# Seven edits to a two-block transformer kernel on one core: the head, the transition, a skipped branch, the convolution's tap matrices

## The chip, the cores and the metric

The kernel runs on one core of one Trainium2 chip. A core has five engines with instruction streams of their own: TensorE (PE, matmuls and transposes; PEld is its weight load), VectorE (DVE), ScalarE (ACT), GpSimd (POOL) and SyncE (SP, which here only issues DMAs). They meet at semaphores. Matrices come from HBM by DMA into SBUF; matmul results stand in PSUM. The metric is the device time of one execution in microseconds (us); lower is better. Before the change three runs gave 1420.13, 1415.26 and 1418.39 us, median 1418.39 us.

## What is computed

All of it is float32 on 256 tokens of width 1024. The first block is a recurrent mixer and a block attention side by side, a cross attention to a memory of 256 rows, and a mixture of 32 experts of which each token takes two. The second block has a retention mixer, a feed-forward layer (FFN), a causal depthwise convolution between two dense matrices, and a second FFN:

```
h = rmsnorm(x, norm_mix); x = x + mixers(h @ w_in) @ w_out
x = x + memory_cross_attention(rmsnorm(x, norm_xattn), rmsnorm(mem, mem_norm), ...)
x = x + hierarchical_moe(rmsnorm(x, norm_ffn), ...)        # 32 experts, 6 MB each
x = rmsnorm(x, norm_final)
h = x; h = h + retention_pool_mixer(rms_norm(h), ...)
h = h + swiglu(rms_norm(h), gate, up, down)
h = h + conformer_conv(rms_norm(h), ...)                   # 31 taps per channel, then layer norm and silu
h = h + swiglu(rms_norm(h), ...); return rms_norm(h)
```

## The kernel before

Every dense product is done as three products of a split: a value is kept as `hi` (rounded) plus `lo` (the rest), and hi·hi, lo·hi and hi·lo are summed in PSUM. A weight piece of 1 MB is loaded into a place `raw` (L270), ACT writes its high half `whi` (L305) and DVE its low half `wlo` (L307); a place is loaded again when both are done. SP issues all weight loads in program order from one queue, so a load that waits for its place holds those behind it.

Most of the program is ordered by a scheduler; in regions marked `manual_schedule` the order on the named engines is the order in which the code is written, and `issue_after(x)` puts an instruction behind x.

- **The head** (`start`, L449 to L543). PE does 24 matmuls on zeros, then waits for the first normed input. Four pieces of `x` (2 token tiles `tt`, 2 column halves `c`) are squared on ACT and DVE (`rstd`); POOL multiplies them by the gain (L512); DVE does a reciprocal root in some twenty small steps (`rsqrt`, L208 to L223); ACT (tt 0) and DVE (tt 1) multiply by it (L472, L474); PE transposes (L480), ACT and DVE split (L484, L488), and the first products follow (L502).
- **The transition** (`cross`). While PE ends the mixer's output product `r` (L436 to L438), POOL multiplies `x` by the gain (L1128), the memory `m` by its gain (L1145) and writes two low halves of `w_kv_x` (L307); DVE does the root of m's norm; DVE scales m's first tile (L1147), ACT the second (L1148); PE then transposes m (L1133).
- **The experts** (`experts`, `overflow`). The 192 MB of expert weights stream through some fifteen places. Behind expert 7 every engine reads a count from SBUF and branches (L1631, L1632): if any expert has over 32 tokens, `overflow` redoes the rest, with loads `ow` on SP's queue (L1434, L1436). In the timed run the branch skips it.
- **Tap matrices** (`conv_weights`, L1926). One POOL instruction writes the 128x6144 tile `w` with which PE does six of the eight channel blocks of the convolution. It stands ahead of `ffn(0)`.
- **Entries** (`enter`): how each of the three later layers starts. Behind the last products of the layer before, `add(c, tt)` adds a quarter of the result to `x` (L1041) and multiplies it by the gain into `xg` (L1042), both on DVE; PE transposes `xg` (L1048), and the first products (`first`, L421) follow. The low halves of the layer's first weight are written by POOL, as is one of the second weight.
- **The convolution** (`conformer`). DVE adds up two channel blocks, tap by tap (L1961); PE does the other six (L2050). Sums over channels of values and squares go through `both` on DVE (L1987) to `sums` on PE (L1974); mean and scale follow, then `centred` (L2077), the scale (L2091), silu and the split.

Of the kernel before, what the change touches and what calls it, by code (L numbers as in the profile page):

```python
# [12 lines left out]
OP = mybir.AluOpType  # L13
# [134 lines left out]
class Block:  # L148
# [298 lines left out]
    def start(self):  # L447
# [57 lines left out]
        with self.tc.manual_schedule(engines={DVE, ACT, POOL, PE}):  # L505
            idle = self.gs.tile([128, 128], F32, name="idle")
            nc.vector.memset(idle, 0.0)
            self.warm(24, idle)
            for c in range(2):
                for tt in range(2):  # L510
                    s = slice(c * 512, (c + 1) * 512)
# [6 lines left out]
            wlow(0, 2)  # L518
            t0, t1 = turned(0, 0), turned(1, 0)
            high(t0, 0, 0)  # L520
            high(t1, 1, 0)
            low(t0, 0, 0)
            low(t1, 1, 0)
            wlow(2, 2)
            scale(0, 1)
            scale(1, 1)
# [12 lines left out]
            wlow(4, 4)  # L539
            products(4, 1, 0, last=True)  # L540
# [485 lines left out]
    def enter(self, g, now, then, *rooms):  # L1026

        nc, x = self.nc, self.x
        products, py, early = self.left
        w = self.halves(0, self.load(now), by=nc.gpsimd)  # L1030
        raw = self.load(then)
# [7 lines left out]
        def add(c, tt):  # L1039
            xs = x[:, tt, half(c)]  # L1040
            nc.vector.tensor_tensor(xs, xs, py[c][tt], op=OP.add)  # L1041
            nc.vector.tensor_tensor(xg[:, tt, half(c)], xs, g[:, half(c)], op=OP.mult)  # L1042

# [20 lines left out]
        with self.tc.manual_schedule(engines={PE, ACT, DVE, POOL}):  # L1064
# [17 lines left out]
            products(1, 1)  # L1082
            add(1, 1)
            turn(1, 0)
# [25 lines left out]
    def cross(self):  # L1110
        nc, i, c = self.nc, self.i, self.c
        self.marks = [self.loads[n].ins for n in (-6, -4)]
        last = self.los[-2].ins
        with self.tc.issue_after(self.loads[-4].ins):
# [27 lines left out]
        with self.tc.manual_schedule(engines={PE, ACT, DVE, POOL}):  # L1142
            gained(0, nc.gpsimd)
            rs = self.rstd(m, after=last)
            nc.gpsimd.tensor_tensor(m[:, 1], m[:, 1], gm, op=OP.mult)  # L1145
            w = self.halves(0, wm, by=nc.gpsimd)
            nc.vector.scalar_tensor_tensor(m[:, 0], m[:, 0], rs[:, 0:1], gm, op0=OP.mult, op1=OP.mult)  # L1147
            nc.scalar.activation(m[:, 1], m[:, 1], AF.Copy, scale=rs[:, 1:2])  # L1148
            t = [turned(m, j, tt) for j in range(2) for tt in range(2)]
            for n in range(4):  # L1150
                high(t[n], hm, n // 2, n % 2)
            for n in range(4):
                low(t[n], hm, n // 2, n % 2)
            gained(1, nc.gpsimd)
# [3 lines left out]
            self.part_cols(w, hm, pm, 0, 0, 0)  # L1158
            self.part_cols(w, hm, pm, 0, 0, 1)
# [266 lines left out]
    def overflow(self):  # L1426
# [3 lines left out]
        def load(src, n):  # L1430
            w = self.ye.tile([128, 2048], F32, name="ow", tag="ye")[:, 0:1024].rearrange("p (k c) -> p k c", k=n)
            if n == 8:
                for a in range(2):
                    nc.sync.dma_start(out=w[:, 4 * a:4 * a + 4], in_=src[a * 512:(a + 1) * 512].rearrange("(p k) c -> p k c", k=4))  # L1434
# [435 lines left out]

    def ffn(self, layer):
        nc, i = self.nc, self.i
# [18 lines left out]
        for f in range(n):  # L1891
# [10 lines left out]
            nc.scalar.activation(s, s, AF.Silu)  # L1902
            nc.gpsimd.tensor_tensor(s, s, rb, op=OP.mult)  # L1903
            nc.vector.tensor_tensor(s, s, pu, op=OP.mult)
# [20 lines left out]
    def conv_weights(self):  # L1925

        shape = [128, 32 * len(BY_PE), 32]
        self.w4 = self.wc.tile(shape, F32, name="w4")
        self.nc.gpsimd.tensor_tensor(self.w4, self.v("w_taps").unsqueeze(2).to_broadcast(shape),
                                     self.c("rep4")[:, None].to_broadcast(shape), op=OP.mult)  # L1930

    def conformer(self):
# [70 lines left out]
        with self.tc.manual_schedule(engines={DVE, ACT, POOL}):  # L2003
# [35 lines left out]
            w4 = self.w4.rearrange("p (b q g) c -> p b q g c", b=len(BY_PE), q=8)  # L2039
            some(99)  # L2040
            w2 = self.pieces(self.rows_of("conv_w_pw2_2", 0))
            made = []
            for n, b in enumerate(BY_PE):
                left = len(BY_PE) - 1 - n
                ps = self.bank("cv")[:, 0:256]
                if not left:
                    moments(total, first=True)
# [4 lines left out]
                if not left:  # L2052
                    moments(pair)
                nc.scalar.activation(dw[:, b], ps, AF.Identity, bias=v("b_dw", b))
                pair = dw[:, b], squared(b)
                if left > 1:
                    add([pair])
                if left == 2:
                    add([(dw[:, d], squared(d)) for d in BY_DVE])
                    made += self.halves(*next(w2))  # L2060
# [18 lines left out]
        with self.tc.manual_schedule(engines={PE, DVE, ACT, POOL}):  # L2079
# [7 lines left out]
            biased(1)  # L2087
            centred(0, 2)
            for b0, n in ((0, 1), (1, 1), (2, 2), (4, 2), (6, 2)):
                s = slice(b0, b0 + n)  # L2090
                nc.vector.tensor_tensor(dw[:, s], dw[:, s], scale[:, None].to_broadcast([128, n, 256]), op=OP.mult)  # L2091
                for b in range(b0, b0 + n):
                    nc.scalar.activation(dw[:, b], dw[:, b], AF.Silu, scale=v("ln_g", b), bias=v("ln_b", b))
                if b0 and b0 < 6:
                    centred(b0 + n, 2)
                nc.scalar.activation(hi[:, s], dw[:, s], AF.Copy)
# [3 lines left out]
    def run(self):  # L2100
# [41 lines left out]
        with ExitStack() as c0:  # L2142
# [33 lines left out]
            with ExitStack() as c2:  # L2176
                self.pools(c2, wc=1)
                self.conv_weights()
                with ExitStack() as c1:
                    self.pools(c1, ffa=2)  # L2180
                    self.ffn(0)
# [79 lines left out]
```

## Time and profile before

| | |
|---|---|
| median of three runs | 1418.39 us |
| profiled execution | 1419.03 us, its span 1417.2 us |
| PE, PEld | 1235.8 us busy (87%), 1058.7 us (75%) |
| DVE, ACT, POOL | 741.5 us (52%), 517.2 us (36%), 170.1 us (12%) |
| DMA | 360.19 MB, mean 254 GB/s; 418 to 419 GB/s through most of the expert stage |
| mean granted PE clock | 0.925 |

The stages by the timeline: head 0 to 27.7 us, mixers to 281, cross attention and routing to 355, experts to about 805, retention to 915, FFN to 1100, convolution to 1215, second FFN to 1405, end at 1417. In the profile a busy share is a mean over stages with unlike limits; a row of the timeline names in brackets how long its engine had been idle, and for whom. A granted clock of 1.00 is TensorE at 2.4 GHz, 0.50 at 1.2 GHz.

### The profile page before, as it was taken

The numbers are of one execution on the slowest core, as the hardware profiler recorded it, in microseconds if no ns is written. First come the engines' busy times: TensorE is split into PE (matmuls) and PEld (weight loads), VectorE is DVE, ScalarE is ACT, GpSimd is POOL, SyncE is SP. The second block draws the span as 40 slices with busy tenths as digits, with TensorE's granted clock in tenths as the row PEclk, the third lists the DMA queues.
The fourth block names the chain that finished last, engine by engine and source line by source line (L and its number), as shares of the span: only waits on it lengthen the run. The fifth ranks groups of instructions, "written<-read, shape, count | busy, mean of one in ns | idle before, by whom it ended". The sixth has DMA issues, their size and how long they took to land. (4 is left out here: it accounts for less than half of the span.)

```text
span 1417.2 us, 29773 instructions
## 1 busy us (share of the span) xinstructions
PE 1235.8 (87%) x12864; PEld 1058.7 (75%) x12864; DVE 741.5 (52%) x1460; ACT 517.2 (36%) x802; POOL 170.1 (12%) x132
## 2 busy tenths in 40 slices
PE   7999999999886477776766799799999998999997
PEld 7989889798765355453544498699999975899996
DVE  5487547866332122121222686765555895755555
ACT  4554533454221111111111464344444424544443
POOL 2022201312000000000000220511111200211112
PEclk8999989999998787687788899899999998999999
DMA  6535514996999899999999985355556186655620
GB/s 207 154 120 170 154 39 146 353 368 246 403 418 415 361 418 418 419 419 419 419 418 419 379 307 186 112 197 195 182 179 187 52 203 204 209 179 180 192 90 30
DMA packets 146460, 360.19 MB, mean 254 GB/s; under 512 B 6672, under 2 KB 101904, under 8 KB 121744
## 3 DMA queue, kind: packets, MB, share of 16 engines
q1 hardware_dynamic: 144800, 353.69, 68.0%
q0 software_dynamic: 1376, 4.25, 1.0%
q8 instruction: 103, 1.69, 0.5%
q14 instruction: 37, 0.30, 0.1%
q10 hardware_dynamic: 144, 0.26, 0.0%
HBM read 354.92 MB, written 3.26 MB: 253 GB/s over the span
## 5 line engine op out<-in xcount | busy, mean ns | idle before, releaser
L307 DVE TENSOR_TENSOR wlo<-raw,whi 128x1024 fp32r<-128x1024 f32 x231 | 297.0, 1291 | 193.2 <-ACT whi L305 190.0
L305 ACT ACTIVATE whi<-raw 128x1024 fp32r<-128x1024 f32 x242 | 254.6, 1058 | 319.7 <-issue 77.4
L1539 PE MATMUL gu<-raw,xe 128*32 128x128 f32 x4096 | 164.2, 308 | 51.0 <-DMA raw<-in_w_exp_up_dram 26.5
L1539 PEld LDWEIGHTS gu<-raw,xe 128*32 128x32 f32 x4096 | 128.9, 121 | 86.7 <-DMA raw<-in_w_exp_up_dram 34.1
L1563 DVE SCALAR_TENSOR_TENSOR ye<-dn,gs,ye 32x256 fp32r<-32x256 f32 x128 | 61.5, 481 | 149.0 <-ACT ye L1562 148.4
L1554 PE MATMUL dn<-raw,ht 128*32 128x256 f32 x1024 | 82.2, 451 | 60.2 <-DMA raw<-in_w_exp_down_dram 37.8
L1562 ACT ACTIVATE ye<-dn,gs 32x256 fp32r<-32x256 f32 x128 | 59.7, 466 | 184.2 <-PE dn L1554 109.2
L1554 PEld LDWEIGHTS dn<-raw,ht 128*32 128x32 f32 x1024 | 34.9, 123 | 94.0 <-DMA raw<-in_w_exp_down_dram 31.0
L413 PE MATMUL fu<-hT,whi 128*128 128x256 f32 x352 | 99.7, 283 | 0.0
L414 PE MATMUL fu<-hTl,whi 128*128 128x256 f32 x352 | 99.6, 283 | 0.0
L415 PE MATMUL fu<-hT,wlo 128*128 128x256 f32 x352 | 99.6, 283 | 0.0
L413 PE MATMUL fg<-hT,whi 128*128 128x256 f32 x320 | 90.6, 283 | 0.0
L415 PE MATMUL fg<-hT,wlo 128*128 128x256 f32 x320 | 90.5, 283 | 0.0
L414 PE MATMUL fg<-hTl,whi 128*128 128x256 f32 x320 | 90.5, 283 | 0.0
L1903 POOL TENSOR_TENSOR fs<-fs,r 128x512 f32<-128x512 f32 x22 | 38.5, 1750 | 302.6 <-ACT fs L1902 302.6
L438 PE MATMUL f<-wlo,fa 128*128 128x512 f32 x176 | 69.2, 393 | 0.0
L436 PE MATMUL f<-whi,fa 128*128 128x512 f32 x176 | 68.9, 391 | 0.0
L437 PE MATMUL f<-whi,fa 128*128 128x512 f32 x176 | 68.7, 391 | 0.0
L413 PEld LDWEIGHTS fu<-hT,whi 128*128 128x128 f32 x352 | 67.1, 190 | 0.0
L414 PEld LDWEIGHTS fu<-hTl,whi 128*128 128x128 f32 x352 | 67.0, 190 | 0.0
L415 PEld LDWEIGHTS fu<-hT,wlo 128*128 128x128 f32 x352 | 67.0, 190 | 0.0
L1620 ACT ACTIVATE hd<-gu,scale 128x128 f32<-128x128 f32 x32 | 11.8, 368 | 144.2 <-PE gu L1539 144.2
(620 smaller groups left out, 2846.8 us busy)
## 6 DMA issues: line engine op xcount, KB each, us to landing
raw<-in_w_exp_gate_dram SPq DMA_DIRECT2D x64, 1024.0 KB, 19.9
raw<-in_w_exp_up_dram SPq DMA_DIRECT2D x64, 1024.0 KB, 19.9
raw<-in_w_exp_down_dram SPq DMA_DIRECT2D x63, 1024.0 KB, 19.9
raw<-in_ffn_w_gate_dram SPq DMA_DIRECT2D x22, 1024.0 KB, 5.4
raw<-in_ffn_w_up_dram SPq DMA_DIRECT2D x22, 1024.0 KB, 5.4
raw<-in_ffn_w_down_dram SPq DMA_DIRECT2D x22, 1024.0 KB, 5.0
raw<-in_w_in_dram SPq DMA_DIRECT2D x20, 1024.0 KB, 5.5
raw<-in_conv_w_pw_dram SPq DMA_DIRECT2D x12, 1024.0 KB, 5.5
```

What stands on the lines that cost most here:

```text
L305: nc.scalar.activation(hi, raw[:, k:k + step], AF.Copy)
L307: self.los.append(eng.tensor_tensor(lo, raw[:, k:k + step], hi.bitcast(F32), op=OP.subtract))
L413: nc.tensor.matmul(ps[:, cb], lhsT=whi[:, k, s], rhs=hi[:, k0 + k], start=f, stop=False)
L414: nc.tensor.matmul(ps[:, cb], lhsT=whi[:, k, s], rhs=lo[:, k0 + k], start=False, stop=False)
L415: nc.tensor.matmul(ps[:, cb], lhsT=wlo[:, k, s], rhs=hi[:, k0 + k], start=False, stop=l)
L436: nc.tensor.matmul(ps[tt], lhsT=hi[:, k0 + k, s], rhs=whi[:, k, cols], start=f, stop=False)
L437: nc.tensor.matmul(ps[tt], lhsT=lo[:, k0 + k, s], rhs=whi[:, k, cols], start=False, stop=False)
L438: nc.tensor.matmul(ps[tt], lhsT=hi[:, k0 + k, s], rhs=wlo[:, k, cols], start=False, stop=l)
L1539: nc.tensor.matmul(pg[quarter(n), at:at + 128], lhsT=xe[:, 4 * kh + k], rhs=w[:, k, n // 2, n % 2], start=(at == kh == k == 0), stop=(at > ...
L1554: nc.tensor.matmul(pd[n % 2][quarter(n), 0:256], lhsT=ht[:, quarter(2 * half + k)], rhs=wd[:, k, n * 256:(n + 1) * 256], start=(half + k = ...
L1562: nc.scalar.activation(hi, part, AF.Copy, scale=gs[q])
L1563: nc.vector.scalar_tensor_tensor(lo, part, gs[q], hi.bitcast(F32), op0=OP.mult, op1=OP.subtract)
```

## The change

1. Head: POOL's four gain products and the two kinds of scale become one DVE instruction for each piece, `x * rs * g`; the low halves of the first weight move behind those of the input.
2. Entries: the first weight's second pair of halves (rows 4 to 8) is issued behind the last `add`, ahead of POOL's low half of the second weight.
3. Transition: the gain products, m's gain and the low halves of `w_kv_x` go from POOL to DVE; both tiles of m are scaled on DVE (`scaled`); the root moves ahead of the last two low halves of `w_out`.
4. Overflow: the loads `ow` go from SP's queue to POOL's.
5. Tap matrices: six POOL instructions of 128x1024, one behind POOL's product in each of the steps 2 to 7 of `ffn(0)`.
6. Convolution: two of the ten adds into `both` stand among the taps of the second channel block.
7. `centred` for three of the four block pairs stands ahead of the first scale.

```diff
@@ start: scale(tt, c)
-            if tt:
-                nc.vector.tensor_scalar(xn[:, tt, s], xn[:, tt, s], rs[:, tt:tt + 1], None, op0=OP.mult)
-            else:
-                nc.scalar.activation(xn[:, tt, s], xn[:, tt, s], AF.Copy, scale=rs[:, tt:tt + 1])
+            nc.vector.scalar_tensor_tensor(xn[:, tt, s], self.x[:, tt, s], rs[:, tt:tt + 1], g[:, s], op0=OP.mult,
+                                           op1=OP.mult)
...
-                    nc.gpsimd.tensor_tensor(xn[:, tt, s], self.x[:, tt, s], g[:, s], op=OP.mult)
@@ enter
-        w = self.halves(0, self.load(now), by=nc.gpsimd)
+        of = self.load(now)
+        w = self.halves(0, of[:, 0:4], by=nc.gpsimd)
...
-            add(1, 1)
+            with self.tc.issue_after(add(1, 1)):
+                w += self.halves(4, of[:, 4:8], by=nc.gpsimd)
@@ cross
-        last = self.los[-2].ins
+        last, end = self.los[-3].ins, self.los[-1].ins
...
-            gained(0, nc.gpsimd)
             rs = self.rstd(m, after=last)
-            nc.gpsimd.tensor_tensor(m[:, 1], m[:, 1], gm, op=OP.mult)
-            w = self.halves(0, wm, by=nc.gpsimd)
-            nc.vector.scalar_tensor_tensor(m[:, 0], m[:, 0], rs[:, 0:1], gm, op0=OP.mult, op1=OP.mult)
-            nc.scalar.activation(m[:, 1], m[:, 1], AF.Copy, scale=rs[:, 1:2])
+            with self.tc.issue_after(end):
+                self.scaled(m, rs, gm, m)
+            gained(0, nc.vector)
...
+            rest(*w[0])
+            gained(1, nc.vector)
+            rest(*w[1])
+            self.part_cols(w, hm, pm, 0, 0, 0)
@@ overflow: load
-                nc.sync.dma_start(out=w, in_=src.rearrange("(k p) c -> p k c", p=128))
+                nc.gpsimd.dma_start(out=w, in_=src.rearrange("(k p) c -> p k c", p=128))
@@ ffn
+            if f > 1:
+                with self.tc.issue_after(scaled.ins):
+                    next(beside, None)
@@ conformer
-            some(99)
...
+                some((8, 10, 99)[min(n, 2)])
...
-            centred(0, 2)
+            for b0 in (0, 2, 4):
+                centred(b0, 2)
```

PE's stream keeps its order but for the transition, where the eight transposes of `xg` move behind the first eight products of m. DVE in the transition before, from the adds of the last quarter of the mixer's result (`x<-x,r`) to m's low halves (`mTl`):

```order
L1011 TENSOR_TENSOR x<-x,r 128x512
L307 TENSOR_TENSOR wlo<-raw,whi 128x1024
L1011 TENSOR_TENSOR x<-x,r 128x512
L307 TENSOR_TENSOR wlo<-raw,whi 128x1024 x3
L210 TENSOR_SCALAR rstd<-ms 128x2
...
L222 SCALAR_TENSOR_TENSOR rstd<-rs,rstd 128x1 x2
L1147 SCALAR_TENSOR_TENSOR raw<-raw,rstd 128x1024
L1011 TENSOR_TENSOR x<-x,r 128x512 x2
L1140 TENSOR_TENSOR mTl<-tr,mT 128x4x128 x4
```

In this order the root (L210 to L222) stands behind four low halves, and one tile of m is scaled behind it. DVE in the same place now (L368 is the scaling of m, L1124 the gain product):

```order
L1005 TENSOR_TENSOR x<-x,r 128x512
L307 TENSOR_TENSOR wlo<-raw,whi 128x1024
L210 TENSOR_SCALAR rstd<-ms 128x2
...
L222 SCALAR_TENSOR_TENSOR rstd<-rs,rstd 128x1 x2
L307 TENSOR_TENSOR wlo<-raw,whi 128x1024 x2
L368 SCALAR_TENSOR_TENSOR raw<-raw,rstd 128x1024 x2
L1005 TENSOR_TENSOR x<-x,r 128x512
L1124 TENSOR_TENSOR raw<-x,raw 128x512
L1005 TENSOR_TENSOR x<-x,r 128x512
L1124 TENSOR_TENSOR raw<-x,raw 128x512
L1136 TENSOR_TENSOR mTl<-tr,mT 128x4x128 x4
```

The root stands two low halves earlier, both tiles of m are scaled right behind the last low half, and two gain products (L1124) have come in ahead of m's low halves; two low halves and two more gain products follow these.

SP at the branch before (the body goes on for some 570 loads):

```order
L279 DMA raw<-in_w_exp_gate_dram 128x2048 x2
L279 DMA raw<-in_w_exp_up_dram 128x2048 x2
L1631 TENSOR_LOAD chosen
L1632 COMPARE_AND_BRANCH
L1434 DMA ow<-in_w_exp_gate_dram 128x4x128 x2
```

The body's loads stand here in SP's stream, behind its branch. SP at the same branch now:

```order
L279 DMA raw<-in_w_exp_up_dram 128x2048 x2
L1634 TENSOR_LOAD chosen
L1635 COMPARE_AND_BRANCH
L1635 UNCONDITIONAL_BRANCH x2
L1634 ISA x2
L279 DMA raw<-in_w_exp_down_dram 128x2048 x2
```

SP still reads the count and branches, over an empty body; the loads stand in POOL's stream.

POOL from the retention (`v`) to the convolution's first step before:

```order
L1848 TENSOR_TENSOR v_17726<-v_17726,row 128x1024
L1929 TENSOR_TENSOR w_18228<-vec,cst 128x6144
L307 TENSOR_TENSOR wlo<-raw,whi 128x1024 x3
L1903 TENSOR_TENSOR fs<-fs,r 128x512 x11
L307 TENSOR_TENSOR wlo<-raw,whi 128x1024
```

The long instruction (L1929) stands ahead of the FFN's first low halves. POOL in the same place now:

```order
L1851 TENSOR_TENSOR v_17721<-v_17721,row 128x1024
L307 TENSOR_TENSOR wlo<-raw,whi 128x1024 x3
L1907 TENSOR_TENSOR fs<-fs,r 128x512 x3
L1939 TENSOR_TENSOR w_18741<-vec,cst 128x1024
L1907 TENSOR_TENSOR fs<-fs,r 128x512
L1939 TENSOR_TENSOR w_18741<-vec,cst 128x1024
...
L1907 TENSOR_TENSOR fs<-fs,r 128x512 x3
L307 TENSOR_TENSOR wlo<-raw,whi 128x1024
```

The one long instruction is gone from its place ahead of the FFN's low halves; six short ones stand each behind one of the FFN's products.

## Rows read from the trace of the kernel before

**Rows 1.** Waits of PE, whole run: engine, line, waited for: us, times, longest.
```profile
PE dn L1554 <- DMA raw<-in_w_exp_down_dram: 37.8, 34, 2.7
...
PE sums L1974 <- DVE both L1987: 4.8, 1, 4.8
...
PE tr L1133 <- DVE raw L1147: 3.7, 1, 3.7
```
**Rows 2.** Windows: us; busy us (instructions) of PE, PEld, DVE, ACT, POOL; PEclk, DMA, GB/s.
```profile
12.00:14.00 2.00, 0.00 (x0) 0.00 (x0) 2.00 (x3) 0.00 (x0) 2.00 (x3) 0.81 1.09 348
14.00:23.00 9.00, 6.12 (x27) 5.72 (x28) 5.47 (x14) 4.60 (x7) 1.60 (x4) 0.50 0.64 174
...
450.00:460.00 10.00, 9.35 (x254) 7.93 (x246) 4.00 (x23) 0.73 (x2) 0.00 (x0) 1.00 1.01 419
475.00:485.00 10.00, 0.71 (x8) 0.52 (x12) 1.72 (x4) 1.48 (x4) 0.00 (x0) 0.50 0.56 215
...
902.00:904.00 2.00, 2.00 (x7) 1.52 (x6) 1.38 (x2) 0.00 (x0) 0.00 (x0) 0.50 1.02 354
...
991.00:1008.00 17.00, 17.00 (x123) 16.00 (x122) 9.33 (x9) 7.40 (x8) 1.82 (x1) 1.00 0.56 186
```
**Rows 3.** Timeline of the head: start us, us, engine, line, what [idle before <-releaser].
```profile
9.29 0.17 DVE L210 TENSOR_SCALAR rstd<-ms 128x2 int32<-128x2 int32 x1
...
9.87 4.92 POOL L512 TENSOR_TENSOR xn<-x,row 128x512 f32<-128x512 f32 x4 [6.34 <-DMA row<-in_norm_mix_dram]
...
15.42 0.72 ACT L474 ACTIVATE xn<-xn,rstd 128x512 f32<-128x512 f32 x1 [3.53 <-DVE rstd L222]
...
16.20 1.97 PE L480 MATMUL tr<-cst,xn 128*128 128x128 f32 x8 [6.99 <-ACT xn L474]
...
26.69 1.12 PE L502 MATMUL u<-hT,wlo 128*128 128x256 f32 x8
```
**Rows 4.** Timeline of the convolution: a root with POOL idle, then the centring.
```profile
1187.78 0.17 DVE L210 TENSOR_SCALAR rv<-var 128x2 int32<-128x2 int32 x1
...
1189.63 0.68 DVE L2077 TENSOR_TENSOR dw<-dw,along 128x512 f32<-128x512 f32 x1
...
1191.99 0.42 DVE L2091 TENSOR_TENSOR dw<-dw,along 128x256 f32<-128x256 f32 x1 [1.68 <-PE along L396]
```
**Rows 5.** Timeline of the transition, DVE and POOL.
```profile
277.12 2.39 DVE L210 TENSOR_SCALAR rstd<-ms 128x2 int32<-128x2 int32 x1
...
283.39 1.28 DVE L1147 SCALAR_TENSOR_TENSOR raw<-raw,rstd 128x1024 f32<-128x1024 f32 x1
...
276.25 5.62 POOL L307 TENSOR_TENSOR wlo<-raw,whi 128x1024 fp32r<-128x1024 f32 x2 [1.27 <-ACT whi L305]
```
**Rows 6.** Instructions of the branch's line: count, ns min/median/max, first and last start us.
```profile
L1632 SPq EVENT_SEMAPHORE  x8: 17/17/17, 467.2 to 481.8; - x8
L1632 POOLq COMPARE_BRANCH  x1: 53/53/53, 360.9 to 360.9; - x1
```
**Rows 7.** Timeline, end of the retention.
```profile
885.99 10.56 POOL L1929 TENSOR_TENSOR w<-vec,cst 128x6144 f32<-128x6144 f32 x1 [24.36 <-DVE ret L1855]
...
886.65 10.97 DVE L307 TENSOR_TENSOR wlo<-raw,whi 128x1024 fp32r<-128x1024 f32 x1
...
898.28 0.79 PE L437 MATMUL r<-whi,ccTl 128*128 128x512 f32 x1 [8.85 <-DVE ccTl L326]
```
**Rows 8.** Timeline of two entries, the first FFN's and the convolution's.
```profile
910.62 2.41 POOL L307 TENSOR_TENSOR wlo<-raw,whi 128x1024 fp32r<-128x1024 f32 x1 [0.28 <-PE tr L1048]
911.06 1.29 DVE L1052 TENSOR_TENSOR hTl<-tr,hT 128x512 fp32r<-128x512 f32 x2 [3.13 <-ACT hT L1049]
...
1104.69 0.63 PE L1048 MATMUL tr<-cst,xg 128*128 128x128 f32 x4 [1.22 <-DVE xg L1042]
...
1117.70 0.28 DVE L222 SCALAR_TENSOR_TENSOR rstd<-rs,rstd 128x1 f32<-128x1 f32 x2
...
1118.90 0.60 PE L396 MATMUL along<-cst,rstd 128*128 128x128 f32 x4
```

More of the change, by code (lines that the diff above doesn't have):

```diff
@@ L508, in start @@
             self.warm(24, idle)
-            for c in range(2):
-                for tt in range(2):
-                    s = slice(c * 512, (c + 1) * 512)
-                    nc.gpsimd.tensor_tensor(xn[:, tt, s], self.x[:, tt, s], g[:, s], op=OP.mult)
             rs = self.rstd(self.x)
@@ L517, in start @@
             whigh(2, 2)
-            wlow(0, 2)
             t0, t1 = turned(0, 0), turned(1, 0)
@@ L521, in start @@
             high(t1, 1, 0)
+            scale(0, 1)
+            scale(1, 1)
             low(t0, 0, 0)
             low(t1, 1, 0)
+            wlow(0, 2)
             wlow(2, 2)
-            scale(0, 1)
-            scale(1, 1)
             whigh(4, 4)
@@ L1041, in add @@
             nc.vector.tensor_tensor(xs, xs, py[c][tt], op=OP.add)
-            nc.vector.tensor_tensor(xg[:, tt, half(c)], xs, g[:, half(c)], op=OP.mult)
+            return nc.vector.tensor_tensor(xg[:, tt, half(c)], xs, g[:, half(c)], op=OP.mult).ins
         def turn(c, tt):
@@ L1142, in cross, with rest @@
         with self.tc.manual_schedule(engines={PE, ACT, DVE, POOL}):
-            gained(0, nc.gpsimd)
             rs = self.rstd(m, after=last)
-            nc.gpsimd.tensor_tensor(m[:, 1], m[:, 1], gm, op=OP.mult)
-            w = self.halves(0, wm, by=nc.gpsimd)
-            nc.vector.scalar_tensor_tensor(m[:, 0], m[:, 0], rs[:, 0:1], gm, op0=OP.mult, op1=OP.mult)
-            nc.scalar.activation(m[:, 1], m[:, 1], AF.Copy, scale=rs[:, 1:2])
+            with self.tc.issue_after(end):
+                self.scaled(m, rs, gm, m)
+            gained(0, nc.vector)
+            w = [(k, *[self.hl.tile([128, 4, 256], F32R, name=n, tag="hl") for n in ("whi", "wlo")]) for k in (0, 4)]
+            for k, hi, _ in w:
+                nc.scalar.activation(hi, wm[:, k:k + 4], AF.Copy)
+            def rest(k, hi, lo):
+                nc.vector.tensor_tensor(lo, wm[:, k:k + 4], hi.bitcast(F32), op=OP.subtract)
             t = [turned(m, j, tt) for j in range(2) for tt in range(2)]
@@ L1153, in cross @@
                 low(t[n], hm, n // 2, n % 2)
-            gained(1, nc.gpsimd)
+            rest(*w[0])
+            gained(1, nc.vector)
+            rest(*w[1])
+            self.part_cols(w, hm, pm, 0, 0, 0)
             t = [turned(xg, 0, tt) for tt in range(2)]
@@ L1433, in load @@
                 for a in range(2):
[L1434 removed]
+                    nc.gpsimd.dma_start(out=w[:, 4 * a:4 * a + 4], in_=src[a * 512:(a + 1) * 512].rearrange("(p k) c -> p k c", k=4))
             else:
[L1436 removed]
+                nc.gpsimd.dma_start(out=w, in_=src.rearrange("(k p) c -> p k c", p=128))
             return w
@@ L1869, in retention, with ffn @@
         self.rows_but_last("mix_w_out_2", (hi, lo), order=-1)
-    def ffn(self, layer):
+    def ffn(self, layer, beside=iter(())):
         nc, i = self.nc, self.i
@@ L1902, in ffn @@
             nc.scalar.activation(s, s, AF.Silu)
-            nc.gpsimd.tensor_tensor(s, s, rb, op=OP.mult)
+            scaled = nc.gpsimd.tensor_tensor(s, s, rb, op=OP.mult)
+            if f > 1:
+                with self.tc.issue_after(scaled.ins):
+                    next(beside, None)
             nc.vector.tensor_tensor(s, s, pu, op=OP.mult)
@@ L1925, in conv_weights @@
     def conv_weights(self):
[L1927 to L1930, printed above, removed]
+        shape = [128, 32, 32]
+        self.w4 = self.wc.tile([128, 32 * len(BY_PE), 32], F32, name="w4")
+        for n in range(len(BY_PE)):
+            s = slice(32 * n, 32 * n + 32)
+            self.nc.gpsimd.tensor_tensor(self.w4[:, s], self.v("w_taps")[:, s].unsqueeze(2).to_broadcast(shape),
+                                         self.c("rep4")[:, None].to_broadcast(shape), op=OP.mult)
+            yield
     def conformer(self):
@@ L2045, in conformer @@
                 ps = self.bank("cv")[:, 0:256]
-                if not left:
-                    moments(total, first=True)
                 for q in range(8):
@@ L2052, in conformer @@
                 if not left:
+                    moments(total, first=True)
                     moments(pair)
+                some((8, 10, 99)[min(n, 2)])
                 nc.scalar.activation(dw[:, b], ps, AF.Identity, bias=v("b_dw", b))
@@ L2057, in conformer @@
                     add([pair])
+                if n == 2:
+                    add([(dw[:, d], squared(d)) for d in BY_DVE])
                 if left == 2:
-                    add([(dw[:, d], squared(d)) for d in BY_DVE])
                     made += self.halves(*next(w2))
@@ L2093, in conformer @@
                     nc.scalar.activation(dw[:, b], dw[:, b], AF.Silu, scale=v("ln_g", b), bias=v("ln_b", b))
-                if b0 and b0 < 6:
-                    centred(b0 + n, 2)
+                if b0 == 2:
+                    centred(6, 2)
                 nc.scalar.activation(hi[:, s], dw[:, s], AF.Copy)
@@ L2177, in run @@
                 self.pools(c2, wc=1)
-                self.conv_weights()
                 with ExitStack() as c1:
                     self.pools(c1, ffa=2)
-                    self.ffn(0)
+                    self.ffn(0, self.conv_weights())
                 self.show("h2", self.x)
```

1 line of the change is left out of this document (removed).

## The prediction

> **What bounds the kernel now.** I read the mean over the whole run first (PE 87% busy, granted clock 0.925), then PE's waits by line [rows 1]: about half of the standing time is the experts' many small waits for weights, such as 34 of at most 2.7 us for the down matrix. Second the windows [rows 2]: at 450 to 460 the DMA share is full and it moves 419 GB/s, so there bytes set the time and a shorter PE gives nothing, but every moment in which the DMA stands is lost. In a step of an FFN (991 to 1008) PE is busy 17.00 of 17.00 us at clock 1.00 and DMA at 0.56: there PE's work sets the time. Head, transition and retention's end are chains: PE stands and its clock falls to 0.50 behind the stop. Third the timelines of the places that the diff touches, for who is waited for. Five places carry the sum; each is a stop of PE or of the DMA, and a shift of PE's stream ahead of the experts is carried through them, since their places for weights are full by then.
>
> **Head (edit 1).** The root runs on DVE from 9.29; ACT's scale can start at 15.42 [rows 3], 6.1 us later. POOL's four gain products (4.92 us in all, 9.87 to 14.8) lie beside it. The same small steps with POOL idle begin at 1187.78 and have made room at 1189.63 for the next DVE instruction [rows 4]: 1.85 us. So the products hold the root up; without them it ends at 11.2. In the new form DVE does one instruction of about 0.68 us (the 128x512 in [rows 4]) for each piece, and PE's first transpose needs the first: 11.2 + 0.7 = 11.9 in place of 16.20, 4.3 earlier. PE then has stood 2.7 us and not 7.0. Its clock fell at about 13.2 (0.81 over 12 to 14 is 0.6 of it at full and the rest at half), 4.0 after it stopped; so it now starts at 2.4 GHz, and of the 6.12 busy us of 14 to 23, all at 0.50 [rows 2], half goes: 3.0. Against that DVE does four scales in place of two, and later low halves and loads stand closer behind PE: 1.3 taken off as an estimate (two instructions of 0.68). 4.3 + 3.0 − 1.3 = **6.0** faster. The head's last products then end at 27.8 − 6 = 21.8 or a little sooner [rows 3]. Bounds: 3.4 if the clock falls all the same and some more is lost behind it, 7.2 if the DVE work is all covered.
>
> **Entries (edit 2).** In the convolution's entry POOL's low halves hold back `xg`, and PE waits 1.22 [rows 8]; the second half now comes behind the last `add`, so this goes: −1.2. But POOL's two instructions of 2.41 [rows 8] now stand back to back there, beside DVE's small norm steps. These start up to 1.9 later by that; from their end (1117.70 + 0.28) to PE's use at 1118.90 are 0.9 [rows 8], so +1.0 in the convolution, and about +0.3 in each FFN, where I put the room at 1.6, an estimate. −1.2 + 1.0 + 2 × 0.3 = **+0.4**, slower. Bounds: −1.2 (only the gain) and +3 (one POOL instruction of 2.41 on the path once, and a little in the others).
>
> Beside POOL's 910.62 instruction of 2.41 DVE's two `hTl`, which read `tr` from PSUM, took 1.29 together from 911.06 on [rows 8], so they did not wait. The Trainium skill (SBUF — State Buffer, Who interferes with whom) says that DVE and GpSimd share one pair of ports as an exclusive lock, that a DVE instruction with two SBUF inputs contends with a GpSimd one that reads SBUF, and that whoever issues first holds it for its whole length. The trace agrees on `hTl`; `tr` is no SBUF input. By that rule the norm's steps and `xg` wait and the split doesn't, which speaks against this edit as the +1.0 does; if the split waited as well, each entry would lose one more POOL half, 2.4 × 3 = 7 us.
>
> **Transition (edit 3).** PE waits 3.7 for m's scale [rows 1], which starts at 283.39, because DVE's root began at 277.12 with an instruction of 2.39 us beside two POOL low halves of 5.62 in all [rows 5], where it takes 0.17 [rows 4]. In the change those low halves are DVE's own and come later, the root stands two low halves earlier, and the scale of m is due by about 279, before PE ends `r` near 281. The wait goes: 3.7, less 0.1 for the hand-over that stays: **−3.6**. Added to DVE are four gain products (0.68 each) and two low halves (1.3 each): 5.3 us behind m's scale, hidden by PE's products of m, which the moved transposes of `xg` let go first. Bounds: −3.9, and if that cover is gone −3.7 + 5.3 = +1.6, or +2.8 with m's second scale (1.28, [rows 5]) uncovered too.
>
> **Branch (edit 4).** While SP skips the body it passes eight semaphore steps from 467.2 to 481.8 [rows 6], each for its own DMA queue, and issues no load. The window 475 to 485 shows 215 GB/s against 419 [rows 2]: (419 − 215) / 419 × 10 = 4.9 us of transfers not done, in a stage that the transfers set. POOL, with no load of the body on it, passed the same line at 360.9 with a branch of 53 ns and no such step [rows 6]. In the change SP has the empty body and POOL the steps, some hundred microseconds before SP's place is reached, where nothing in the stage needs POOL. **−4.9**. Bounds: −1 (the drain comes back in part as a later wait for a place), −4.9; 0 if SP keeps the steps.
>
> **Tap matrices (edit 5).** POOL's 10.56 us instruction at 885.99 holds a low half of DVE for 10.97 us, and PE stands 8.85 for `ccTl` until 898.28 [rows 7]; the window at 902 to 904 still has the clock at 0.50 [rows 2], and of the 5.7 us from 898.28 to 904, matmuls throughout, half is lost: 2.8. The low half alone takes 1.28 (as the scale of its size, [rows 5]), so the stop all but goes: 8.85 + 2.8 = 11.6, **−11.5**. Bounds: −8.8 (the stop alone), −12. The six new instructions are 10.56 / 6 = 1.76 each. In an FFN step of 17.00 us DVE is busy 9.33 and POOL 1.82 [rows 2], so 7.7 us of room cover a piece: 0, at most +1 over the six if a low half comes late.
>
> **Convolution (edits 6, 7).** The number of DVE instructions up to the last `both` is the same, only their order differs; so PE's 4.8 us for `both` [rows 1] stays: 0. Three centrings (0.68 each, 2.0) move into a gap that ends at 1191.99 and has 1.68 of idle after the one at 1189.63 [rows 4]; later steps wait on ACT all the same: 0. Bounds of both: −0.7 and +0.7 (one such instruction).
>
> **Sum.** −6.0 + 0.4 − 3.6 − 4.9 − 11.5 = −25.6. The profiled execution took 1419.0 (1.8 of it outside the span of 1417.2), so 1393.4; it is 0.6 above the median of the runs, so **1393 us**.
>
> **Rivals.**
> - *The branch's bubble stays* (SP still has the steps, or the transfers drained there were needed for a wait that comes anyway). For: an engine must catch up on what the skipped loads would have signalled. Against: POOL's clean pass [rows 6]. Gain 20.7: 1398.
> - *The head gains only its front.* The clock falls at once in the new stop too, or DVE's four scales come late; the transition gives half. For: PE starts cold behind a stop of any length that I haven't seen at this place. Against: 3.7 us of stop in the transition [rows 1] left the clock alone. Gain 25.6 − 2.6 − 1.8 = 21.2, or 18 with the lower bound of the entries: 1398 to 1401.
> - *The tap matrices don't pay.* Next to the low half stands a wait for the weights (the DMA share is 1.02 at 902 to 904 [rows 2]); PE waits for that in place of the POOL. Gain of the part 2 to 4: 1401 to 1403.
> - *Slower.* Each of the six pieces stands right behind POOL's 1.82 us product, so POOL holds DVE for 3.6 us in a step that now has 1.8. Should PE run into the low halves so held, it stops 3.6, and pays half-clock behind the stop as behind 898 (2.8): 6.4 × 6 = 38, against 25.6 gained: 1419 + 38 − 26 = 1431. It decides from 25.6 / 6 = 4.3 us for each piece. Against: DVE's 7.7 us of room in such a step and PE's unbroken 17.00 [rows 2].
> - *It doesn't do what it says*: for the convolution's edits that is my forecast already.
>
> **How the numbers follow.** Forecast 0.62, branch 0.13, head 0.12, tap matrices 0.07, slower 0.03; the last 0.03 for small remains of several gains, within 0.3% of before (4 us, about what a measurement here can tell from no change). The forecast's own range is 1388 to 1399 (the bounds of head and entries on one side, all gains full on the other); with the branch, the head and most of the tap matrices it is 1384 to 1404. Faster 0.94, same 0.03, slower 0.03.
>
> **What would show it.** Head: first `tr` near 12, last `u` of the head ending near 21, clock 1.00 through 14 to 23; wrong if the root is still long. Transition: no wait of `tr` of m for DVE. Branch: no semaphore steps on SP, DMA at 419 GB/s throughout; wrong if they stand there. Tap matrices: no low half near 11 us, clock 1.00 at 886 to 905 on before's scale, FFN steps of 17.0. Entries: PE's 1.2 gone, a new one near 1 at `along`. Convolution: `sums` still 4.8. If PE's waits in the second FFN's or first FFN's steps grow, the forecast is wrong.

## The result and the profile after

The changed kernel took 1395.35 us (median of 4 runs, 1394.03 to 1398.24); the kernel before, on the same chip, 1419.26. The ratio is 0.9835 with a 95% interval of 0.9802 to 0.9867, so 19 to 28 us faster. The forecast was 1393. Ratios leave out one slow execution of the last kernel below (1922.69 us, at a mean granted clock of 0.552 where the others have 0.93). The profiled execution took 1396.49, its span 1394.7 (before 1417.2). PE is busy 88% of it (1233.5 us of work, 2 less than before), POOL 151 us (before 170).

Where the 22.5 us came from is read best by stages. The cuts are the first starts of named matmuls in each timeline (the end of the last one where the table says so); a stage that no edit touches should keep its length.

| stage, from - to | before | after | difference | forecast |
|---|---|---|---|---|
| head, 0 - first `q` | 27.65 | 21.10 | −6.55 | −6.0 |
| mixers, to the end of the last `r` | 253.41 | 252.40 | −1.0 | 0 |
| transition, to the first `xs` | 31.23 | 27.44 | −3.8 | −3.6 |
| cross attention, to the first `lg` | 32.57 | 32.57 | 0 | 0 |
| routing, to the first `xe` | 10.82 | 13.99 | **+3.2** | 0 |
| experts, to the first `tr` of `xg` | 450.47 | 447.08 | −3.4 | −4.9 |
| retention up to its first `r` | 71.82 | 71.88 | 0 | 0 |
| retention's end and entry, to the first `fu` | 44.49 | 32.80 | −11.7 | −11.5 and +0.3 |
| FFN and entry, to the first `cg` | 190.69 | 190.72 | 0 | −0.2 |
| convolution, to its first `r` of `zT` | 80.40 | 80.88 | +0.5 | 0 |
| entry and second FFN, to the end of its last product | 215.27 | 215.41 | +0.1 | +0.3 |

Head, the kernel after, rows of the timeline (start, us, engine, line, what) that answer to [rows 3]:

```profile
8.17 0.17 DVE L210 TENSOR_SCALAR rstd<-ms 128x2 int32<-128x2 int32 x1
...
10.06 2.74 DVE L471 SCALAR_TENSOR_TENSOR xn<-x,rstd,row 128x512 f32<-128x512 f32 x4
10.92 1.26 PE L478 MATMUL tr<-cst,xn 128*128 128x128 f32 x8 [1.91 <-DVE xn L471]
12.87 2.08 PE L500 MATMUL u<-hT,whi 128*128 128x256 f32 x8 [0.69 <-ACT hT L482]
...
20.14 1.12 PE L500 MATMUL u<-hT,wlo 128*128 128x256 f32 x8
```

The root begins 1.1 us sooner than before because the last piece of `x` landed sooner in this execution, and now takes 1.9 us, not 6.1 (8.17 to the first scale at 10.06). Three windows of it (us, busy us of PE, PEld, DVE, ACT, POOL, clock, DMA share, GB/s):

```profile
12.00:13.00 1.00, 0.31 (x3) 0.13 (x1) 1.00 (x3) 1.00 (x3) 0.00 (x0) 0.91 1.09 348
13.00:16.00 3.00, 3.00 (x14) 3.00 (x15) 2.19 (x4) 0.93 (x2) 0.00 (x0) 0.50 1.12 250
16.00:18.00 2.00, 2.00 (x19) 2.00 (x18) 0.69 (x1) 0.96 (x3) 0.00 (x0) 0.94 1.03 261
```

The clock still falls, near 12.8, but for some 3.4 us and not for 10 (the first eight `u` take 2.08, the last 1.12). Among the nine profiles of kernels with edit 1 and 24 matmuls this is one of the two better ones: in the other seven the clock fell between 10.8 and 12.1, ahead of or among the first eight transposes (1.7 to 2.0 us in place of 1.26), and came back 6.8 us later.

Transition, the kernel after, DVE and PE, as in [rows 5]:

```profile
264.45 0.16 DVE L210 TENSOR_SCALAR rstd<-ms 128x2 int32<-128x2 int32 x1
...
269.96 2.48 DVE L368 SCALAR_TENSOR_TENSOR raw<-raw,rstd 128x1024 f32<-128x1024 f32 x2
...
273.33 1.91 PE L1129 MATMUL tr<-cst,raw 128*128 128x128 f32 x16
```

The root's first instruction takes 0.16 in place of 2.39, m is scaled by 272.4, and the transposes carry no wait in brackets. The branch's line, as in [rows 6] (count, ns, first and last start), and windows in the form of [rows 2]:

```profile
L1635 POOLq EVENT_SEMAPHORE  x4: 17/43/43, 355.9 to 356.1; - x4
...
L1635 SPq COMPARE_BRANCH  x1: 50/50/50, 453.8 to 453.8; - x1
```
```profile
337.00:344.00 7.00, 7.00 (x14) 3.42 (x14) 5.49 (x46) 1.55 (x6) 1.23 (x1) 0.51 1.01 424
350.00:355.00 5.00, 5.00 (x104) 4.74 (x106) 0.66 (x5) 0.83 (x2) 0.00 (x0) 1.00 0.23 70
460.00:470.00 10.00, 4.66 (x97) 2.75 (x97) 1.67 (x4) 1.40 (x3) 0.00 (x0) 1.00 1.02 420
...
877.00:886.00 9.00, 9.00 (x42) 7.43 (x41) 6.07 (x7) 3.44 (x4) 1.40 (x1) 1.00 0.43 130
...
931.00:948.00 17.00, 17.00 (x123) 15.99 (x122) 10.35 (x9) 7.52 (x8) 3.70 (x3) 1.00 0.57 186
```

POOL passes its semaphore steps at 356 within a microsecond, SP has none, and behind its branch DMA goes on at 420 GB/s. Gone with them is the longest stop of PE in the kernel before, 17.2 us at this branch: ACT there waited 22.78 us for SP, and PE, by way of DVE, for ACT.

```profile
481.89 0.47 ACT L1562 ACTIVATE ye<-dn,gs 32x256 fp32r<-32x256 f32 x1 [22.78 <-SPq L1632]
```
```profile
PE dn L1554 <- DVE ht L1547: 19.5, 3, 17.2
```

The stage is only 3.4 us shorter: for the first 8 us of that stop, to 475, the transfers went on at 418 GB/s, and over 475 to 485 still at 215 [rows 2]. The first two of the windows above are what the forecast did not have: at 337 to 344 PE is busy without a gap at half clock, and at 350 to 355 the DMA stands (70 GB/s). The fourth is the place of PE's 8.85 us stop [rows 7], now full at clock 1.00; the last is an FFN step with a piece of the tap matrices in it, still 17.00 of 17.00. The low half there and a piece (DVE, POOL):

```profile
875.15 1.21 DVE L307 TENSOR_TENSOR wlo<-raw,whi 128x1024 fp32r<-128x1024 f32 x1
...
931.75 1.92 POOL L1939 TENSOR_TENSOR w<-vec,cst 128x1024 f32<-128x1024 f32 x1
```

The residual's products `y` at the routing, the kernel after:

```profile
337.87 6.68 PE L1362 MATMUL y<-x,cst 128*128 128x512 f32 x8
```

In the kernel before the same eight began at 348.85 and took:

```profile
348.85 3.68 PE L1359 MATMUL y<-x,cst 128*128 128x512 f32 x8
```

Their order and operands are the same; only the clock is not. And the entry of the convolution, the kernel after, as in [rows 8]:

```profile
1082.43 5.22 POOL L307 TENSOR_TENSOR wlo<-raw,whi 128x1024 fp32r<-128x1024 f32 x2 [4.33 <-ACT whi L305]
...
1082.86 2.53 DVE L1037 TENSOR_TENSOR xg<-x,raw 128x512 f32<-128x512 f32 x1
1085.31 1.27 DVE L1047 TENSOR_TENSOR hTl<-tr,hT 128x512 fp32r<-128x512 f32 x2
...
1085.53 0.63 PE L1043 MATMUL tr<-cst,xg 128*128 128x128 f32 x4 [1.09 <-DVE xg L1037]
```

The wait has moved from the second quarter of `xg` (1.22) to the fourth (1.09). `sums` still waits 4.8 for `both`.

### The profile page after: what moved, and what is told of

Its sections match the earlier page's. It is cut to its first block, busy times and chain, and to the rows that moved or that the text cites. A ratio compares the mean times of both kernels' runs of the same rounds, so it can differ in the third digit from the quotient of the medians.

```text
span 1394.7 us, 29759 instructions
## 1 busy us (share of the span) xinstructions
PE 1233.5 (88%) x12864; PEld 1053.2 (76%) x12864; DVE 735.6 (53%) x1469; ACT 514.9 (37%) x799; POOL 151.3 (11%) x126
## 3 DMA queue, kind: packets, MB, share of 16 engines
q1 hardware_dynamic: 144800, 353.69, 68.4%
## 4 chain that ended last, share of the span: by engine, by line
PE 53%; DMA 29%; DVE 4%; ACT 1%; issue 1%; SPq 0%; ACTq 0%; DVEq 0%
DMA raw<-in_w_exp_up_dram 10%; DMA raw<-in_w_exp_down_dram 10%; DMA raw<-in_w_exp_gate_dram 9%; PE fu L413 3%; PE fu L414 3%; PE fu L415 3%; PE f L438 3%; PE f L436 3%; PE f L437 3%; PE fg L415 3%; PE fg L413 3%; PE fg L414 3%; PE r L436 2%; PE r L437 2%; PE r L438 1%; PE gu L1542 1%
## 5 line engine op out<-in xcount | busy, mean ns | idle before, releaser
L307 DVE TENSOR_TENSOR wlo<-raw,whi 128x1024 fp32r<-128x1024 f32 x231 | 292.4, 1270 | 189.7 <-ACT whi L305 186.2
L1557 PE MATMUL dn<-raw,ht 128*32 128x256 f32 x1024 | 85.1, 462 | 46.9 <-DMA raw<-in_w_exp_down_dram 42.6
L1624 DVE SCALAR_TENSOR_TENSOR hd<-gu,scale,hd 128x128 f32<-128x128 f32 x32 | 11.2, 350 | 105.8 <-ACT hd L1623 105.7
```

The lines of the kernel that those rows point to most:

```text
L307: self.los.append(eng.tensor_tensor(lo, raw[:, k:k + step], hi.bitcast(F32), op=OP.subtract))
L1557: nc.tensor.matmul(pd[n % 2][quarter(n), 0:256], lhsT=ht[:, quarter(2 * half + k)], rhs=wd[:, k, n * 256:(n + 1) * 256], start=(half + k = ...
```

## The experiments

My theory was that the parts add up place by place; the rival for each, that the experts' transfers or a neighbour give it back. One stretch stayed open from the comparison of the profiles: the routing. Each kernel was timed beside the kernel before on one chip; the ratio is to that. The kernel before took 1415.93, 1418.37 and 1416.85 us there (1419.26 beside the changed kernel), so ratios and stages are compared, not times. "Undone" kernels are the changed kernel with one edit taken back.

**Edit 1 undone.**
```diff
-            scale(0, 1)
-            scale(1, 1)
+            for c in range(2):
+                for tt in range(2):
+                    nc.gpsimd.tensor_tensor(xn[:, tt, s], self.x[:, tt, s], g[:, s], op=OP.mult)
...
```


> The changed kernel with edit 1 (the head) undone. By the sum of terms the head's gain stays through the experts: 5.3 to 6.5 us slower than the changed kernel's 1395.4, so about 1401, and PE's first transposes near 16 instead of 10.9. Rival: the expert stage is set by the weight transfers, so an earlier start only fills the places sooner and is given back there: 1395 to 1397.

1400.38 us, ratio 0.9875 (0.9846 to 0.9904). PE's wait at the first transposes is back:

```profile
PE tr L480 <- ACT xn L474: 6.9, 1, 6.9
```

`q` begins at 27.11, and the 6.0 us to the profile after are still 6.5 at the experts' start and 6.7 at their end. So in these two profiles the shift is carried through the experts, against the rival. The times alone would not decide it: the four runs spread from 1395.57 to 1403.11, and the interval overlaps the changed kernel's (0.9802 to 0.9867).

**Edit 3 undone.**
```diff
-            with self.tc.issue_after(end):
-                self.scaled(m, rs, gm, m)
-            gained(0, nc.vector)
+            gained(0, nc.gpsimd)
+            nc.gpsimd.tensor_tensor(m[:, 1], m[:, 1], gm, op=OP.mult)
+            w = self.halves(0, wm, by=nc.gpsimd)
...
```


> The changed kernel with edit 3 (the transition) undone. By the sum: PE waits some 3.7 us for m's scale again and 1.2 us more at the end of the mixer's product, 1399 to 1400.5. Rival: the start of the experts is set by transfers, not by PE: 1395 to 1397.

1399.83, ratio 0.9882 (0.9866 to 0.9899), with the old wait:

```profile
PE tr L1129 <- DVE raw L1143: 3.7, 1, 3.7
```

The stage takes 32.4 us against 27.4: edit 3 is worth 4.9 here, 3.8 against the profile before (31.2). The kernel with edit 5 alone, whose code up to here is that of before, took 32.4 as well: behind the same stop of 3.7 us the clock fell to 0.50 for 3.4 us in these two profiles and not in that of before. Edit 3 undone:

```profile
281.00:285.00 4.00, 4.00 (x24) 4.00 (x23) 3.54 (x6) 3.17 (x6) 2.42 (x2) 0.57 1.03 423
```

In the kernel before the same place stands at

```profile
285.00:289.00 4.00, 3.81 (x33) 3.42 (x32) 3.82 (x7) 3.26 (x6) 2.51 (x2) 1.00 1.03 416
```

Another wait is back in the mixers' stage, of `r` for a low half of `w_out` (0.8 in the kernel before, none in the kernel after):

```profile
PE r L438 <- DVE wlo L307: 0.9, 1, 0.9
```

**Edit 4 undone.**
```diff
-                nc.gpsimd.dma_start(out=w, in_=src.rearrange("(k p) c -> p k c", p=128))
+                nc.sync.dma_start(out=w, in_=src.rearrange("(k p) c -> p k c", p=128))
```


> The changed kernel with edit 4 undone (the skipped loads on SP's queue again). By the sum: eight semaphore steps on SP, a hole of 4.9 us in the transfers, 1400. Rival: half of the hole is given back because the places are full for a while anyway: 1396.5 to 1398.

1397.25, ratio 0.9866 (0.9837 to 0.9895). SP's eight steps and the hole are back:

```profile
L1635 SPq EVENT_SEMAPHORE  x8: 17/17/17, 459.4 to 473.0; - x8
```
```profile
470.00:475.00 5.00, 0.00 (x0) 0.00 (x0) 0.82 (x2) 0.93 (x2) 0.00 (x0) 0.50 0.35 113
```

(419 − 113) / 419 × 5 = 3.7 us of transfers are missing, but the experts take 449.6 us against 447.1, only 2.5 more. The interval can't tell 1397 from 1400; the stage lengths speak for the rival: a part of the hole is given back. Against the two kernels with this edit whose routing took the same 12.3 us (446.8 and 447.5, edits 3 and 5 undone) it is 2.0 to 2.7. The traces show where it goes. In the last 20 us of the stage, two windows of 10 us, the profile after moves

```profile
774.58:784.58 10.00, 6.76 (x117) 4.25 (x113) 7.24 (x22) 1.67 (x4) 0.00 (x0) 0.67 0.99 397
784.58:794.58 10.00, 7.74 (x64) 3.11 (x60) 5.06 (x12) 5.16 (x10) 0.75 (x2) 0.85 0.88 295
```

and the kernel with the hole

```profile
777.35:787.35 10.00, 5.71 (x113) 3.62 (x112) 7.53 (x22) 2.03 (x5) 0.00 (x0) 0.81 1.01 416
787.35:797.35 10.00, 7.76 (x64) 3.11 (x60) 4.91 (x11) 5.16 (x10) 0.74 (x2) 0.85 0.98 329
```

Against 419 GB/s the first lacks 3.5 us of transfers there and the second 2.2: 1.3 us of what the closed hole gains is lost again at the stage's end. The other traces agree: 2.1 to 2.2 us in the three with the hole, 3.3 to 3.5 in the eleven without.

**Edit 5 undone; edit 5 alone on the kernel before; edit 5 uncut.** The third keeps the place (behind POOL's product in step 2 of the first FFN) but not the cut:
```diff
-        for n in range(len(BY_PE)):
-            s = slice(32 * n, 32 * n + 32)
-            self.nc.gpsimd.tensor_tensor(self.w4[:, s], ...)
-            yield
+        self.nc.gpsimd.tensor_tensor(self.w4, ...)
+        yield
```


> The changed kernel with edit 5 undone (one POOL instruction ahead of the first FFN). By the sum: the stop of 8.9 us and half clock behind it, 11.9 us in all, 1407. Rival: the six pieces cost something in the FFN's steps that comes back here, or the clock is granted all the same: 1403 to 1404.5.

> The kernel before with edit 5 alone (the tap matrices in six pieces inside the first FFN). If the parts are independent: 11.9 us faster than before, a ratio of 0.9916, the stop of 8.9 us gone and nothing else moved. Rival: the part is worth less without the others, 8.8 us, 0.9938.

> The changed kernel, but the tap matrices are one POOL instruction of 128x6144 again, behind POOL's product in step 2 of the first FFN (in place of six pieces in steps 2 to 7). If the cut into pieces matters: POOL holds DVE some 10.6 + 1.8 us in one step in which DVE has 7.7 us of room, so PE stands about 4.5 us there and its clock may fall for 1 to 3 us more: 1400 to 1403. Rival, only the place matters and the FFN's buffers cover it: 1395 to 1396.

Undone: 1405.72, ratio 0.9927 (0.991 to 0.9945). The stop is back, again behind a low half of 10.97 us, and the stage from the retention's first `r` takes 44.07 against 32.80:

```profile
PE r L437 <- DVE ccTl L326: 8.9, 1, 8.9
```

Alone: 1408.05, ratio 0.9942 (0.9923 to 0.9961); this stage takes 32.62, so the whole 11.9 us is there, and the FFN is as long as before (190.68). The times say less: the ratio is 8.2 us, where 11.9 wants 0.9916, just outside the interval, and the rival's 0.9938 lies inside it. Why is open: the profiled execution, the fastest of the four, shows no shortfall (its span is 13.2 us under before's, with the routing at 12.3 and not 10.8, the transition at 32.4 and not 31.2, but the mixers 2.1 shorter), so it can't tell what the other three lacked. Uncut: 1401.04, ratio 0.9884 (0.9865 to 0.9903). The long instruction holds DVE, and PE after it:

```profile
933.51 11.09 DVE L307 TENSOR_TENSOR wlo<-raw,whi 128x1024 fp32r<-128x1024 f32 x1 [1.70 <-ACT whi L305]
```
```profile
PE fg L415 <- DVE wlo L307: 3.6, 1, 3.6
```

That stop and the clock behind it (0.91 over 932 to 949) make the FFN 196.0 us, 5.3 longer. So by the stages the place gives about half of the gain and the cut the rest, by the room of DVE that was read in [rows 2].

**Edit 2 undone; edits 6 and 7 undone.**
```diff
-            with self.tc.issue_after(add(1, 1)):
-                w += self.halves(4, of[:, 4:8], by=nc.gpsimd)
+            add(1, 1)
...
-            for b0 in (0, 2, 4):
-                centred(b0, 2)
+            centred(0, 2)
```


> The changed kernel with edit 2 (the entries) undone. In the changed kernel PE's wait of 1.2 us in the convolution's entry has only changed its place (1.1 us for the fourth quarter of xg), so no difference in time: 1394 to 1396.5, with the wait of 1.2 back and that of 1.1 gone. Rival, the forecast's working (norm steps held, a new wait at along): 0.4 faster without the edit, at most 3.

> The changed kernel with edits 6 and 7 (the convolution's sums and the centring) undone. By the forecast no difference: 1394 to 1396, PE's wait for both still 4.8 us. Rival: the order of sums is worth the 0.6 us by which the changed kernel's depthwise products end sooner, or the centring costs 0.5: within 0.7 either way.

1395.46, ratio 0.9837 (0.9819 to 0.9855), and 1394.70, ratio 0.9837 (0.9815 to 0.9858): neither part can be told from nothing. Without edit 2 the old wait returns in place of the new one:

```profile
1083.26 0.63 PE L1042 MATMUL tr<-cst,xg 128*128 128x128 f32 x4 [1.22 <-DVE xg L1036]
```

**Head: PE kept busy to the transposes.**
```diff
-            self.warm(24, idle)
+            self.warm(36, idle)
```


> The changed kernel with 36 in place of 24 matmuls on zeros at the start, so that PE is busy to about 10.6 instead of 9.0. If the clock's fall at 12.9 comes from PE's stop of 1.9 us ahead of the first transposes, it stays at 1.00 through 13 to 16 and the head ends 1.6 us sooner. Rival: the fall comes from the short stop after the transposes (0.7 us) or from the thin stretch as a whole, and stays: no difference, or 0.3 us slower by the matmuls that stand ahead of the transposes.

1394.07, ratio 0.9837 (0.9814 to 0.986). The clock stays at 1.00 through the head (with the 12 more matmuls PE stands 0.2 us ahead of the transposes, not 1.9):

```profile
12.00:13.00 1.00, 0.93 (x6) 0.69 (x7) 1.00 (x3) 1.00 (x3) 0.00 (x0) 1.00 1.10 346
13.00:16.00 3.00, 2.31 (x20) 2.07 (x19) 3.00 (x6) 2.15 (x4) 0.00 (x0) 1.00 1.11 271
```

From the first transpose to the first `q` it takes 8.7 us against 10.2: 1.5, near the 1.6 expected. By the times they don't reach the end. In the mixers PE stands 3.9 us at one `inv` for nothing that the profile shows ("issue"), 2.1 more than in the profile after:

```profile
169.63 0.26 PE L871 MATMUL inv<-d,vz 32*32 32x32 f32 x2 [3.86 <-issue]
```

The same stop of 3.9 stands in the other kernel with 36 matmuls (below) and in none with 24 (1.1 to 1.8 us there, 0.9 in the kernel before). The traces show what PE waits for: in this one a packet of 16 KB on the queue of the instructions begins at 167.09, 2.5 us before the stop ends, and of all 61 stops of PE of over 1 us in the fourteen traces that are put down to "issue", 60 end 2.3 to 2.6 us behind the start of such a packet (of its 948 other stops of that length 28 do). That points to waits for code, though no run changes the load itself. Why it comes so late with 36 matmuls stays open.

**Routing: no matmuls ahead of the ranks.**
```diff
-        self.warm(7, c("ident"))
```


> The changed kernel without the 14 matmul instructions on the identity (1.7 us) that stand between the residual's products (y from x) and the ranks in the routing. In the changed kernel the clock is 0.50 there, y takes 6.7 us in place of 3.7, and DVE has been done for 2.7 us when PE comes to the ranks. If PE's lateness there is what the experts' start waits for: 1.2 to 1.7 us faster, and the stop of the transfers behind the start is shorter by as much. Rival: the transfers alone set the stage, no difference; or the clock, with PE idle, falls for longer: 1 us slower.

1394.61, ratio 0.9832 (0.9812 to 0.9851). Here `y` took 5.07 us, the routing 11.12 against 13.99, and the experts ended 3.1 us sooner relative to `lg` than in the profile after: in these profiles PE's lateness at the routing is carried through the experts' stage. By the timing it is no difference, so the expected 1.2 to 1.7 is not shown in time.

**The changed kernel once more, and the three ideas together** (36 matmuls, none ahead of the ranks, the entries' second low halves on DVE).
```diff
-                w += self.halves(4, of[:, 4:8], by=nc.gpsimd)
+                w += self.halves(4, of[:, 4:8])
...
```


> The changed kernel as it is, beside the next ones on the same chip, and a second profile of it: 0.9835 of the time before, and at the routing the clock at 0.50 through part of y (5.0 to 7 us in place of 3.7) once more if that stop is a habit of the changed kernel and not of one execution.

> The changed kernel with three more edits: 36 matmuls on zeros at the start, none ahead of the ranks, and in the entries the second pair of low halves on DVE in place of POOL. If the three terms read from the profiles add up (1.5 at the head, 1.5 at the routing, 1.1 in the convolution's entry and up to 1.3 in the second FFN's), 3.5 to 5.5 us faster than the changed kernel, so a ratio of 0.980 to 0.981. Rival: the transfers of the experts swallow the first two and the third moves to another wait: no difference, 0.983 to 0.984.

Again: 1392.68, ratio 0.9824 (0.9809 to 0.9839), and the half clock at the routing once more:

```profile
337.40 6.42 PE L1362 MATMUL y<-x,cst 128*128 128x512 f32 x8
```

Together: 1392.99, ratio 0.9834 (0.9816 to 0.9852); no difference, against my 3.5 to 5.5. The entry in the FFN stage gave 0.7 (190.00), the routing 3.2 (10.83), but the mixers took 255.4 us, 3 more than in the profile after, 2.2 of it in the stop at `inv`:

```profile
170.71 0.26 PE L871 MATMUL inv<-d,vz 32*32 32x32 f32 x2 [3.91 <-issue]
```

So no version here beats the changed kernel beyond the measurement.

## Why the prediction was right, and where not

The time (1393 forecast, 1395.35 measured) and the sign were right, and of the five terms those of the transition and the tap matrices were right in place and mechanism and near in size; the other three less so. That the total came out so near is in part luck: in the profiles the misses of the routing (+3.2) and the branch (+1.5) lie against gains that were not forecast or partly chance (head 0.6, mixers 1.0, of which 0.8 is the wait of `r`, retention's end and entry 0.5).

- **Head, −6.0.** The root without POOL's products took 1.9 us as worked out. Failed: "so it now starts at 2.4 GHz". In the profile after the transposes did, but the clock fell near 12.8 all the same and came back after 3.4 us; in seven of nine profiles it was down for the transposes too and stayed so for 6.8 us. That −6.55 came out is luck: the inputs landed 1.1 us sooner, and the half clock was short. Over the nine profiles of kernels with edit 1 and 24 matmuls `q` begins at 21.1 to 23.4 (median 22.8), over the three without it at 27.1 to 27.7 (27.3): the term is −4.5, between its bounds of 3.4 and 7.2.
- **Entries, +0.4.** The size, nothing, was near; the step failed. I let DVE's norm steps and `along` be late; it is the fourth `xg` that the first of POOL's two low halves holds (2.53 us in place of 0.69): in spite of `issue_after(add(1, 1))` POOL starts 0.4 us ahead of that `xg`. The rule cited from the Trainium skill (SBUF — State Buffer, Who interferes with whom) is borne out by that row: two SBUF inputs wait, while the two `hTl` behind it, with one from PSUM, took 1.27 us as ever.
- **Transition, −3.6.** Measured −3.8 against the profile before, −4.9 by undoing it. The wait is gone, and of the added DVE instructions one low half shows up in PE's waits, for 0.3 us. Two things were missed: the 0.8 us of `r`, gone as well, and the clock. "Left the clock alone" held for the profile before; in two others the same stop cost 1.1 us more by half clock.
- **Branch, −4.9.** The mechanism was right (steps and hole are gone, and come back with the edit undone). The size was too large: the stage is 3.4 us shorter, 2.5 by undoing it. I took the hole's bytes for the time; about 1.3 us of it are given back in the last 20 us of the stage, where the transfers now stand longer. What they wait for there the runs don't show. Nor did I name PE's 17.2 us at this branch, the longest wait of the run, of which 3.4 us or less was worth anything. A reading was wrong too: the eight steps are not each for a DMA queue of its own (353.69 of the 360.19 MB stand on one queue in the trace); each step waits for a load's semaphore, and the last four end as the last four loads land (the last at 481.75, the step at 481.76).
- **Tap matrices, −11.5.** Measured in its stage −11.7, −11.3 by undoing it and −11.9 alone (by the times alone 8.2). The pieces cost nothing: the FFN is 190.7 us in every kernel with the pieces but the last (190.0, by its entry), as it is without them. Pieces of 1.92 and not 1.76 us made no difference, and the rival that DVE's room would be overrun comes true only when the cut is taken away.
- **Convolution, 0.** Undoing both edits moved nothing that can be told from the spread of this stage (78.2 to 80.9 us over the fourteen profiles); `sums` waits 4.8 as forecast.
- **What the sum lacked, +3.2.** The routing. Its eight `y` products ran at half clock in the profile after, and that pushed the experts' start. It needs no edit ahead of it: the kernel with edit 5 alone, whose code is that of before up to the FFN, took 12.3 us in this stage too. Whether the change makes it more frequent is open, since none of the seven profiles with the changed code up to here and all its matmuls shows less than 12.3. Over the fourteen profiles it takes 10.8 (before, and both kernels with 36 matmuls), 11.1 (without the matmuls ahead of the ranks), 12.3 (four kernels) or 14.0 (six); the profile of before had caught the good case. The sum of −25.6 and the measured −22.5 differ by about this much, but only because the other misses nearly cancel.
- **The parts add up**, by the stages. By the ratios the kernels with edit 1, 3, 4 or 5 undone lose 5.7, 6.7, 4.4 and 13 us against 0.9835, 30 in all against some 23 gained; the interval of that 0.9835, 5 us either way, enters four times, so the times neither show nor refute it.

## What to carry to other kernels

Look for a POOL instruction that runs beside DVE on the path: one of 10.6 us cost 11 to 12 us of PE's time, and cut into pieces that fit DVE's room in a loop bound by PE it cost nothing. Put the loads of a branch that is mostly skipped on a queue whose engine reaches the branch early and has nothing in flight; and count a hole in the transfers as an upper bound of what closing it gives: the longest wait of an engine (17.2 us here) says little of what it is worth. Cut profiles into stages by named instructions before comparing two of them: stages that no edit touches show how much of a difference is the clock's or the inputs' (over the fourteen profiles here 250.0 to 255.4 us in the mixers and 10.8 to 14.0 in the routing). One profile can have caught the good case, as that of before did in the transition and the routing, and no edit of 1 to 3 us can be judged by the end time alone.

## What the runs showed of the hardware

- The clock fell while PE had no gap. From 335 to 337 us of the profile after PE is busy 2.00 of 2.00 with narrow products (36 and 72 columns) at 1.00, and from 337 to 344, busy 7.00 of 7.00, the clock is 0.51. The same instructions in the profile before stayed at 1.00.

```profile
335.00:337.00 2.00, 2.00 (x21) 2.00 (x19) 0.80 (x2) 1.91 (x6) 2.00 (x2) 1.00 0.88 365
```

- Skipping a branch took SP 13.6 us over eight semaphore steps (459.4 to 473.0, edit 4 undone) with its own transfers in flight, and POOL 0.2 us over four in the profile after, where none had to land.
- Twenty-four more matmul instructions at the start went with a stop of 3.9 us at one place some 160 us later, in both kernels that have them; like 60 of 61 such stops it ended 2.3 to 2.6 us behind the start of a 16 KB packet of instructions.
